# A first product from the bank behind the head norm's sums, first queries turned in their banks, another order of the low parts and of both layers: a two-layer decoder trunk on one core

## The chip, the core and the metric

One core of a Trainium2 chip. The metric is the device time of one execution in microseconds; before the change the median of three runs is 367.07 us (366.95 to 367.86). Engines are named as in the profile: PE (TensorE, its weight loads PEld), DVE (VectorE), ACT (ScalarE), POOL (GpSimd), SP (the queue that issues the weights' DMAs).

## The reference, cut to what matters

256 tokens of 1024 features go through two layers; each adds a mixer's output, then a gated per-layer embedding.

```python
def rms_norm(x, gain):
    y = xf * lax.rsqrt(jnp.mean(xf * xf, axis=-1, keepdims=True) + NORM_EPS)
def rope(x, pos):
    x1, x2 = xf[..., :half], xf[..., half:]
    return concatenate([x1 * cos - x2 * sin, x2 * cos + x1 * sin])
def moba_layer(h, w_in, q_gain, k_gain, w_out, pos):          # layer 0
    q, k, v, z = split(h @ w_in, 4)
    q = rope(rms_norm(split_heads(q, 16), q_gain), pos)       # a norm per head of 64
    k = rope(rms_norm(split_heads(k, 16), k_gain), pos)
    o = merge_heads(moba_attention(q, k, v)) * silu(z)
    return o @ w_out
def nsa_layer(...):                                           # layer 1
    q, kc, vc, ks, vs, kw, vw, gl, z = split(h @ w_in, offs)
    # q, ks, kw: head norm and rope as above; kc, vc compressed by an MLP;
    # three attention branches (compressed, selected, window), mixed by sigmoid(gl)
for i in range(2):
    x = x + mixer_i(rms_norm(x, norm_gain[i]))
    gate = sigmoid(rms_norm(x, ple_gate_gain[i]) @ ple_w_gate[i])
    x = x + gate * (p[i] @ ple_w_proj[i])
```

## The kernel before, in words

**Products in three parts.** Every float32 matrix is split into a high part rounded to TensorE's fast float32 format (ACT, `hi`; for activations `ah`) and the rest (DVE, `lo` and `al`: raw minus high), and a product is three matmuls: high by high, high by low, low by high (`split` L465, `split_act` L477, `Unit.mul` L506). So each weight tile that SP fetches into one of five `raw` buffers costs one ACT and one DVE instruction before PE can finish its share; the `raw` buffer is free for the next DMA when DVE has made `lo`.

**Layer 0.** The first queries (`uq0`, L750) are computed while x and the first weights arrive: the loop at L765 takes the eight k-tiles x0 to x7. Then `moba_half` (L792) makes keys (`uk`) and values (`uv`) for the first eight heads, and once more queries, keys and values for the other eight; the string HALVES sets in which order these steps are recorded. `qe` and `ke` copy a product out of its PSUM banks by ACT (`rope_evac`), so that the banks come free; `q` and `k` call `rope`. The attention of the first eight heads runs between the second half's products.

**The head norm and rope** (`rope`, L605). ACT squares, DVE sums (`ssq`), DVE adds epsilon (`r0`, shown as r), POOL raises the 128x16 numbers to the power -1/2 (`r_q`, `r_k`), and DVE multiplies by sine and cosine tables: two half products with the halves exchanged into a buffer `qs` (shown as tmp), one full product, one sum per token half t. For queries DVE negates the result (`nr_q`); for keys it multiplies by it. What feeds the products is the PSUM bank (`mm`), or, if an evacuation was recorded, the copy in SBUF (`q`, `k`).

**What sets the order.** Nothing runs in the order of the text: a planner (`Plan`, L85) records all operations with their dependencies, gives each a cost, and lays them out on the engines in list-scheduling order; the program then holds five fixed queues. Earlier recorded operations win among ready ones. HALVES and ORDER (for layer 1: KE and QE0/QE1 are the ropes, KT the transposes and low parts of the keys, vs/vw/kc/q1 projections, S, T, V, A, b, c pieces of the attention of group 0 to 3) set the order of recording; BEHIND tells behind which weight loads the constants' DMAs stand; `hold` keeps an operation behind another's start, and `together` (L219) makes a run of operations stand next to each other.

Of the kernel before, what the change touches and what calls it, by code (L numbers as in the profile page):

```python
# [7 lines left out]
F32 = mybir.dt.float32  # L8
# [5 lines left out]
P = 128  # L14
# [6 lines left out]
NRAW, NHI, NLO, NPT, NA = 5, 5, 5, 9, 9  # L21
WARM = 16
MARGIN = 100.0
ORDER = ("vw vs VS KE KT QE0 0A 0S1 0S0 0T0 0S3 kc 0T1 0S2 0T2 1A 0T3 q1.0 1S0 VW 1T0 1S2 q1.1 KC W0 0V q1.2 W1 "
         "1S3 q1.3 1T3 QE1 2A W2 1T2 W3 1S1 WE 2S2 2S0 0c 1T1 1V 2T2 0b 1c 2T0 3A 2S1 2c 2T1 2S3 3S1 3c 1b 2T3 3S0 "
         "2V 2b 3T0 3T1 3S2 3T2 3S3 3T3 3V 3b")

HALVES = ("k0 consts k1 norm qe k2 k3 v0 tabs masks v1 v2 q v3 k v", "k0 k1 k2 k3 q v0 k v1 v2 v3 v")

BEHIND = "0 3"  # L30
CST, CST_N = {}, 0
for _k, _n in (("ident", 128), ("cos", 128), ("sin", 128), ("mask", 384), ("cmask", 32), ("valid", 2), ("rmask", 4),
               ("cosc", 64), ("sinc", 64), ("repl", 256)):
# [51 lines left out]
class Plan:  # L85
# [77 lines left out]
    def cost(self, op, views, first):  # L163
        n = first.elems() if isinstance(first, View) else 0
        e, m = op.engine, op.method
        if m == "dma_start":
            v = first if isinstance(first, View) else op.args[1]
            return v.elems() * 4 * v.ap.ap[0][1]
        if e == "tensor":
            k, c = op.args[1].ap.ap[0][1], op.args[1].ap.ap[1][1]  # L170
            op.mode = tuple(128 if x > 64 else 64 if x > 32 else 32 for x in (k, c))
            if m == "transpose":
                return 109.2
            if op.args[1].ap.dtype == mybir.dt.bfloat16:
                return n / 2.4
            if op.args[1].ap.dtype == F32R:
                return (n + 32) / 2.4 if n > 128 else 110

            return 2 * max(54.6 if op.mode == (128, 64) else 109.2, 2 * n / 2.4 / (2 if op.mode == (128, 64) else 1))
        if e == "gpsimd":  # L180
            if op.kwargs.get("op") == OP.pow:
                return POW + 130.0 * n
            return 100 + 2.3 * n
        psum = any(self.tags[v.tile.tag]["psum"] for v in views)
        rows = first.ap.ap[0][1]
        half = 110 if rows in (60, 64) and (any(v.box()[0] != first.box()[0] for v in views)
                                            or psum and first.ap.dtype == F32R and m == "activation") else 0
        if e == "scalar":
            if first.tile.tag == "early":
                return 1500.0  # L190
            c = (60 if psum else 110) + 0.833 * max(n, op.args[1].elems())
            return half + c + 93 * sum(isinstance(op.kwargs.get(k), View) for k in ("scale", "bias", "accum_out"))
        if m == "tensor_tensor_reduce":
            return 130 + 1.04 * n
        if m == "reciprocal":
            return 65 + 6.9 * n
        if m == "tensor_reduce":
            return 65 + 1.04 * op.args[1].elems()
        two = len([v for v in views if v.elems() > 2 and v is not first]) > 1
# [197 lines left out]
def trunk(ctx: ExitStack, tc: tile.TileContext, a, out):  # L397
# [14 lines left out]
    def tmp(name):  # L412
        return work.tile([P, 512], F32, tag="tmp", name=name, bufs=5)
# [63 lines left out]
    def split_act(src, gain=None, either=False):  # L477
        hi = apool.tile([P, T], F32R, tag="ah", name="ah")
        lo = apool.tile([P, T], F32R, tag="al", name="al")
        if gain is None:  # L480
            nc.scalar.activation(hi, src, AF.Copy)
            nc.vector.tensor_tensor(lo, src, hi.bitcast(F32), op=OP.subtract)
        else:
            if either:
                nc.copy(hi, src, gain)
            else:
                nc.scalar.activation(hi, src, AF.Copy, scale=gain)
            nc.vector.scalar_tensor_tensor(lo, src, gain, hi.bitcast(F32), op0=OP.mult, op1=OP.subtract)
        return hi, lo
# [115 lines left out]
    def rope(ps, tab, nb, norm, is_q, tag, bufs, o=None):  # L605
        if o is None:
            o = work.tile([P, 2, 512], F32, tag=tag, name=tag, bufs=bufs)
        else:
            ps = [o[:, t] for t in range(2)]
        o = o.rearrange("p t (h d) -> p t h d", d=HD)  # L610
        ssq = work.tile([P, 2, 8], F32, tag="ssq", name="ssq")
        for t in range(2):
            sq = tmp("hsq").rearrange("p (h d) -> p h d", d=HD)
            nc.scalar.activation(sq.rearrange("p h d -> p (h d)"), ps[t], AF.Square)
            nc.vector.tensor_reduce(ssq[:, t], sq, axis=AX.X, op=OP.add)
        r0 = work.tile([P, 2, 8], F32, tag="r0", name="r0")
        for t in range(2):
            nc.vector.tensor_scalar(r0[:, t], ssq[:, t], 1.0 if is_q else 1.0 / HD,
                                    norm.e2[:, 0 if is_q else 1, t:t + 1], op0=OP.mult, op1=OP.add)
        r = work.tile([P, 2, 8], F32, tag="r_" + tag, name="r_" + tag, bufs=bufs)  # L620
        nc.gpsimd.tensor_tensor(r.rearrange("p t h -> p (t h)"), r0.rearrange("p t h -> p (t h)"), neg_half, op=OP.pow)
        if is_q:
            nr = work.tile([P, 2, 8], F32, tag="nr_" + tag, name="nr_" + tag, bufs=bufs)
            nc.vector.tensor_scalar(nr, r, -1.0, None, op0=OP.mult)
        for t in range(2):
            v = ps[t].rearrange("p (b g d) -> p b g d", b=nb, d=HD)
            g = 8 // nb

            def tb(i, lo, hi):
                return tab[:, i, t, :, None, lo:hi].to_broadcast([P, nb, g, hi - lo])  # L630

            qs = tmp("qs").rearrange("p (b g d) -> p b g d", b=nb, d=HD)
            ot = o[:, t].rearrange("p (b g) d -> p b g d", b=nb)
            nc.vector.tensor_tensor(qs[:, :, :, 0:32], v[:, :, :, 32:64], tb(1, 0, 32), op=OP.mult)
            nc.vector.tensor_tensor(qs[:, :, :, 32:64], v[:, :, :, 0:32], tb(1, 32, 64), op=OP.mult)
            nc.vector.tensor_tensor(ot, v, tb(0, 0, HD), op=OP.mult)
            nc.vector.tensor_tensor(ot, ot, qs, op=OP.add)
            if not is_q:
                nc.vector.tensor_tensor(o[:, t], o[:, t], r[:, t, :, None].to_broadcast([P, 8, HD]), op=OP.mult)
        return o, (nr if is_q else None)  # L640
# [121 lines left out]
    nc.scalar.activation(consts.tile([P, 16], F32, name="early"), neg_half, AF.Exp)  # L762
    for o, i in zip(nc.ops[since + 1:], range(since, len(nc.ops))):
        o.after.append(i)
    for k in range(KT):  # L765
        if k:
            nc.sync.dma_start(xT[:, k], a["x"][:, k])
        x0.append(split_act(xT[:, k], ng[:, 0, k:k + 1], k == 0))
        if k == 0:
            ws = [split(None, (1, 256), True, raw) for raw in halves]  # L770
            for part in ((0, 1), (2,)):
                for c, w in enumerate(ws):
                    for b in range(2):
                        uq0.mul(w, 0, 0, b, cols=(256 * c, 256 * c + 256), parts=part)
            continue
        c0, raw = 512 * (k % 2), second if k == 1 else None
        if k >= 4:

            if not c0:
                pair = wpool.tile([P, 1024], F32, tag="raw", name="raw", bufs=NRAW)  # L780
            raw = pair[:, c0:c0 + 512]
            nc.sync.dma_start(raw, a["moba_in"][0, k // 2, :, c0:c0 + 512])
        since = len(nc.ops)
        w = split(a["moba_in"][0, k // 2, :, c0:c0 + 512], (1, 512), small=k < 4, raw=raw)
        if k == 1:

            nc.hold(since, since - 2)
        for b in range(2):
            uq0.mul(w, 0, k, b)
    tab, held_at = [], []  # L790

    def moba_half(h):  # L792
# [11 lines left out]
        def norm():  # L804

            def adds():
                for k in range(KT):
                    n0.add(k)

            nc.hold_on(adds, loads[-1] - 1)  # L810
            n0.finish()

        def tabs():
# [21 lines left out]
        for step in HALVES[h].split():  # L835
            if step in parts:
                parts[step]()
            else:
                loads.append(len(nc.ops))
                {"k": uk, "v": uv}[step[0]].step(int(step[1]))  # L840
# [537 lines left out]
```

## Time and profile before

| | us |
|---|---|
| median of three runs | 367.07 |
| the profiled execution, whole | 367.55 |
| its span, first to last instruction | 365.8 |
| PE busy | 356.0 |
| DVE busy | 324.3 |
| ACT busy | 268.8 |
| POOL busy | 33.7 |

[...] All but a few operations pass through one helper and so carry one line, L375; they are told apart by tile names. Busy time is the union of an engine's instructions, and a matmul's shown duration overlaps the next one's, so for PE the distance from start to start is the price of one.

### The profile page before, as it was taken

How to read it: one execution, taken by the hardware profiler on the slowest of the kernel's cores; microseconds unless marked ns; L12 is line 12 of the kernel's file. 1: busy time of each engine (PE TensorE's matmuls, PEld its weight loads, DVE VectorE, ACT ScalarE, POOL GpSimd, SP SyncE). 2: the span in 40 equal slices, each digit the busy share in tenths (PEclk: the TensorE clock that was granted, in tenths of full speed). 3: DMA queues.
4: the chain of work that ended last, by engine and by line, in shares of the span. 5: the costliest groups of instructions: out<-in, count | busy, mean ns of one | idle time of the engine just before them, and what ended most of it. 6: DMA issues, size and time to landing. Idle time of an engine off the chain costs nothing.

```text
span 365.8 us, 7124 instructions
## 1 busy us (share of the span) xinstructions
PE 356.0 (97%) x2569; PEld 322.0 (88%) x2569; DVE 324.3 (89%) x799; ACT 268.8 (73%) x591; POOL 33.7 (9%) x26
## 2 busy tenths in 40 slices
PE   7998999999999999999999999999999999999994
PEld 5776788789999999999888998877998998999994
DVE  4896999999799987789979999989999999687964
ACT  4874677778688886745944887979976999966711
POOL 1054300330000000010013300003000000000010
PEclk9999999999999999999999999999999999999998
DMA  7985574334732644065364854065775100273102
GB/s 241 341 300 184 212 247 156 107 125 139 265 119 103 211 175 148 28 213 190 96 205 125 282 178 159 18 224 191 276 226 202 64 2 8 109 279 126 58 30 86
DMA packets 20051, 58.97 MB, mean 161 GB/s; under 512 B 2480, under 2 KB 5296, under 8 KB 20016
## 3 DMA queue, kind: packets, MB, share of 16 engines
q1 hardware_dynamic: 19440, 58.04, 46.3%
q10 hardware_dynamic: 576, 0.48, 0.4%
q8 instruction: 20, 0.33, 0.4%
q14 instruction: 15, 0.12, 0.1%
HBM read 57.46 MB, written 1.05 MB: 160 GB/s over the span
## 4 chain that ended last, share of the span: by engine, by line
PE 82%; DVE 8%; DMA 3%; POOL 2%; issue 2%; ACT 1%; SPq 0%; ACTq 0%; DVEq 0%
PE mm L375 61%; PE tr L375 12%; PE s L375 9%; DVE lo L375 2%; POOL r_q L375 2%; DMA xT<-in_x 2%; DMA tmp<-in_moba_in 1%; DVE q L375 1%; ACT hi L375 1%; DVE tmp L375 1%; DVE vcB L375 1%; SPq L375 0%; DVE k_1r L375 0%; DVE kd_0r L375 0%; DVE hl L375 0%
## 5 line engine op out<-in xcount | busy, mean ns | idle before, releaser
L375 DVE TENSOR_TENSOR lo<-raw,hi 128x1024 fp32r<-128x1024 f32 (+2 forms) x100 | 114.4, 1159 | 5.2 <-ACT hi L375 4.8
L375 PE MATMUL mm<-al,hi 128*128 128x256 f32 x416 | 118.2, 286 | 0.0
L375 PE MATMUL mm<-ah,lo 128*128 128x256 f32 x416 | 118.1, 286 | 0.0
L375 PE MATMUL mm<-ah,hi 128*128 128x256 f32 x416 | 117.5, 287 | 0.0
L375 ACT ACTIVATE hi<-raw 128x1024 fp32r<-128x1024 f32 (+2 forms) x100 | 98.2, 1005 | 24.9 <-PE mm L375 15.2
L375 PEld LDWEIGHTS mm<-al,hi 128*128 128x128 f32 x416 | 79.6, 191 | 0.4
L375 PEld LDWEIGHTS mm<-ah,lo 128*128 128x128 f32 x416 | 79.4, 191 | 0.2
L375 PEld LDWEIGHTS mm<-ah,hi 128*128 128x128 f32 x416 | 78.8, 191 | 0.5 <-issue 0.2
L375 PE MATMUL mm<-lo,ah 128*128 128x512 f32 (+2 forms) x178 | 65.3, 376 | 2.3 <-DVE lo L375 2.3
L375 PE MATMUL mm<-hi,ah 128*128 128x512 f32 (+2 forms) x178 | 66.5, 377 | 0.8 <-DVE hi L375 0.6
L375 PE MATMUL mm<-hi,al 128*128 128x512 f32 (+2 forms) x178 | 66.3, 374 | 0.3 <-DVE al L375 0.3
L375 ACT ACTIVATE sm<-sm,nb 128x128 f32<-128x128 f32 (+1 forms) x96 | 42.7, 448 | 7.6 <-DVE nb L375 7.3
L375 PEld LDWEIGHTS mm<-lo,ah 128*128 128x128 f32 x178 | 33.2, 188 | 8.1 <-DVE lo L375 3.3
L375 PEld LDWEIGHTS mm<-hi,ah 128*128 128x128 f32 x178 | 33.6, 190 | 7.0 <-ACT hi L375 0.9
L375 PEld LDWEIGHTS mm<-hi,al 128*128 128x128 f32 x178 | 33.7, 190 | 5.9 <-DVE al L375 0.8
L375 DVE CUSTOM_DVE_ANT_0 sm<-s,cst,nr_q 128x128 f32<-128x128 f32 (+1 forms) x96 | 35.4, 411 | 2.2 <-PE s L375 1.9
L375 POOL TENSOR_TENSOR r_q<-r,neg_half 128x16 f32<-128x16 f32 x5 | 19.8, 3961 | 82.1 <-DVE r L375 82.1
L375 ACT ACTIVATE pt<-tr 128x384 f32<-128x384 f32 x48 | 22.0, 483 | 4.9 <-PE tr L375 4.6
L375 PE MATMUL tr<-cst,sm 128*128 128x128 f32 x144 | 24.4, 277 | 0.0
L375 ACT ACTIVATE ah<-xT,gain_in 128x256 fp32r<-128x256 f32 x31 | 14.4, 498 | 12.5 <-DVE xT L375 9.3
L375 ACT ACTIVATE tmp<-tmp 128x512 f32<-128x512 f32 (+3 forms) x22 | 11.2, 516 | 13.8 <-DVE tmp L375 13.8
L375 POOL TENSOR_TENSOR rstd<-ms,neg_half 128x2 f32<-128x2 f32 x4 | 4.9, 1236 | 176.1 <-DVE ms L375 176.1
(172 smaller groups left out, 545.3 us busy)
## 6 DMA issues: line engine op xcount, KB each, us to landing
raw<-in_moba_in SPq DMA_DIRECT2D x28, 512.0 KB, 4.6
raw<-in_nsa_in SPq DMA_DIRECT2D x24, 512.0 KB, 4.3
raw<-in_w_out SPq DMA_DIRECT2D x16, 512.0 KB, 3.9
raw<-in_ple_gate SPq DMA_DIRECT2D x16, 512.0 KB, 3.6
raw<-in_w SPq DMA_DIRECT2D x8, 512.0 KB, 4.4
raw<-in_ple_proj SPq DMA_DIRECT2D x4, 512.0 KB, 4.5
raw<-in_nsa_vs SPq DMA_DIRECT2D x4, 304.0 KB, 3.1
xT<-in_x SPq DMA_DIRECT2D x8, 128.0 KB, 4.3
```

The source lines that it names most:

```text
L375: getattr(getattr(self.nc, o.engine), o.method)(*[real(x) for x in o.args], **{k: real(x) for k, x in o.kwargs.items()})
```

## The change

1. `rope` records the first exchanged half product of token half 0 (`turn(0, 0)`) together with the two `r0` operations, ahead of POOL's power.
2. HALVES has no `qe` in the first half any more: the first queries are turned from their banks (mm); the second half has `qe` and `ke` (evacuated queries and keys). The eight x steps are now steps of HALVES.
3. In the first eight steps each weight's `lo` is held behind the start of the same step's `al`.
4. The strings HALVES, BEHIND and ORDER are others; the planner's cost of the 128x16 power falls by 1000 ns, which also moves operations. Group 3 adds its compressed branch inside its last products (B instead of b).

```diff
-ORDER = ("vw vs VS KE KT QE0 0A 0S1 0S0 0T0 0S3 kc 0T1 ...
-HALVES = ("k0 consts k1 norm qe k2 k3 v0 tabs masks v1 v2 q v3 k v", "k0 k1 k2 k3 q v0 k v1 v2 v3 v")
-BEHIND = "0 3"
+ORDER = ("KE vs vw KT VS QE0 0A VW 0S1 0S0 0S3 0T1 0T0 0S2 kc 0T2 ...
+HALVES = ("x0 x1 x2 x3 x4 x5 x6 x7 k0 consts norm k1 k2 tabs k3 masks v0 v1 v2 v3 v q k",
+          "k0 k1 qe q k2 k3 v0 ke k v1 v2 v3 v")
+BEHIND = "0 2"
...
             if op.kwargs.get("op") == OP.pow:
-                return POW + 130.0 * n
+                return (POW if n < 16 else 1300.0) + 130.0 * n
...
+        def turn(t, c):
+            lo, hi = 32 * c, 32 * c + 32
+            nc.vector.tensor_tensor(qss[t][:, :, :, lo:hi], vs[t][:, :, :, 32 - lo:64 - lo], tb(1, t, lo, hi), op=OP.mult)
+
+        since = len(nc.ops)
         for t in range(2):
             nc.vector.tensor_scalar(r0[:, t], ssq[:, t], 1.0 if is_q else 1.0 / HD,
                                     norm.e2[:, 0 if is_q else 1, t:t + 1], op0=OP.mult, op1=OP.add)
+
+        turn(0, 0)
+        nc.together(since)
         r = work.tile([P, 2, 8], F32, tag="r_" + tag, name="r_" + tag, bufs=bufs)
         nc.gpsimd.tensor_tensor(r..., r0..., neg_half, op=OP.pow)
...
         for t in range(2):
-            nc.vector.tensor_tensor(qs[:, :, :, 0:32], v[:, :, :, 32:64], tb(1, 0, 32), op=OP.mult)
-            nc.vector.tensor_tensor(qs[:, :, :, 32:64], v[:, :, :, 0:32], tb(1, 32, 64), op=OP.mult)
-            nc.vector.tensor_tensor(ot, v, tb(0, 0, HD), op=OP.mult)
-            nc.vector.tensor_tensor(ot, ot, qs, op=OP.add)
+            if t:
+                turn(t, 0)
+            turn(t, 1)
+            nc.vector.tensor_tensor(ot, vs[t], tb(0, t, 0, HD), op=OP.mult)
+            nc.vector.tensor_tensor(ot, ot, qss[t], op=OP.add)
...
-    for k in range(KT):
+    def first(k):
...
         x0.append(split_act(xT[:, k], ng[:, 0, k:k + 1], k == 0))
+        low = len(nc.ops) - 1
...
+        nc.hold(len(nc.ops) - 1, low)
...
-            nc.hold_on(adds, loads[-1] - 1)
+            nc.hold_on(adds, len(nc.ops) - 1)
```

The amount of work is the same: the program has as many matmuls of every shape as before, and DVE and ACT exchange a few copies (the planner picks the engine for some).

**First place: DVE at the first queries' rope** (layer 0, while PE works on the first keys). lo is the low part of a weight; raw_119, raw_120, raw_116 and raw_117 hold, in this order, the second, third and fourth weight of the first keys and the first weight of the values; mm_78 and mm_79 are the queries' two banks. Before:

```order
L375 TENSOR_SCALAR r_0_137<-ssq_135,e_0_128 128x8 x2
L375 TENSOR_TENSOR tmp_83<-q_131,tq_0_133 128x8x32
L375 TENSOR_TENSOR lo_112<-raw_120,hi_107 128x1024
L375 TENSOR_TENSOR tmp_83<-q_131,tq_0_133 128x8x32
L375 TENSOR_TENSOR tmp_84<-q_131,tq_0_133 128x8x32
L375 TENSOR_TENSOR lo_113<-raw_116,hi_108 128x1024
L375 TENSOR_TENSOR q_131<-q_131,tq_0_133 128x512
L375 TENSOR_TENSOR tmp_84<-q_131,tq_0_133 128x8x32
L375 TENSOR_TENSOR q_131<-q_131,tmp_83 128x512
L375 TENSOR_SCALAR nr_q_141<-r_q_139 128x16
L375 TENSOR_TENSOR q_131<-q_131,tq_0_133 128x512
L375 TENSOR_TENSOR lo_114<-raw_117,hi_109 128x1024
```

With the change (numbers of buffers are shifted by three; raw_123, raw_119 and raw_120 are the keys' third and fourth and the values' first weight):

```order
L376 TENSOR_SCALAR r_0_139<-ssq_137,e_0_128 128x8 x2
L376 TENSOR_TENSOR tmp_83<-mm_78,tq_0_131 128x8x32
L376 TENSOR_TENSOR lo_115<-raw_123,hi_110 128x1024
L376 TENSOR_TENSOR tmp_83<-mm_78,tq_0_131 128x8x32
L376 TENSOR_TENSOR q_135<-mm_78,tq_0_131 128x512
L376 TENSOR_TENSOR tmp_84<-mm_79,tq_0_131 128x8x32
L376 TENSOR_TENSOR q_135<-q_135,tmp_83 128x512
L376 TENSOR_TENSOR lo_116<-raw_119,hi_111 128x1024
L376 TENSOR_SCALAR nr_q_143<-r_q_141 128x16
L376 TENSOR_TENSOR tmp_84<-mm_79,tq_0_131 128x8x32
L376 TENSOR_TENSOR q_135<-mm_79,tq_0_131 128x512
L376 TENSOR_TENSOR lo_117<-raw_120,hi_112 128x1024
```

The products now read the banks instead of the SBUF copy. Between the negation nr_q and the values' first low part stood one full product; now a half product and a full one.

**Second place: DVE in the first steps.** hi_108 is the second weight's high part, lo_113 its low part, al_98 the low part of x1. Before:

```order
L375 CAST hi_108<-tmp_84 128x512
L375 TENSOR_TENSOR lo_113<-tmp_84,hi_108 128x512
L375 SCALAR_TENSOR_TENSOR al_98<-xT_63,gain_in_64,ah_89 128x256
```

With the change:

```order
L376 CAST hi_111<-tmp_84 128x512
L376 SCALAR_TENSOR_TENSOR al_101<-xT_63,gain_in_64,ah_92 128x256
L376 TENSOR_TENSOR lo_116<-tmp_84,hi_111 128x512
```

The low part of x1 goes ahead of the weight's; the steps behind already had this order.

**Third place: DVE at the start of layer 1's attention.** k_0r, k_1r, v_0r (before v_1r) and kd_0r are the keys' low parts of the four groups (each x2), hl the low part of the first group's queries, lo_113 to lo_115 (before) and lo_116 to lo_118 (now) the second to fourth weight of kc. Before:

```order
L375 TENSOR_TENSOR k_0r<-tr_76,k_0r 64x512 x2
L375 TENSOR_TENSOR k_1r<-tr_76,k_1r 64x512 x2
L375 TENSOR_SCALAR nr_q_141<-r_q_140 128x16
L375 TENSOR_TENSOR q_132<-q_132,tmp_83 128x512
L375 TENSOR_TENSOR lo_113<-raw_116,hi_108 128x1024
...
L375 TENSOR_TENSOR lo_115<-raw_118,hi_110 128x1024
L375 TENSOR_TENSOR v_1r<-tr_75,v_1r 64x512 x2
L375 TENSOR_TENSOR kd_0r<-tr_75,kd_0r 64x512 x2
L375 TENSOR_TENSOR hl_149<-tr_76,hl_149 64x512 x2
```

With the change:

```order
L376 TENSOR_TENSOR k_0r<-tr_76,k_0r 64x512 x2
L376 TENSOR_TENSOR k_1r<-tr_76,k_1r 64x512 x2
L376 TENSOR_TENSOR v_0r<-tr_75,v_0r 64x512 x2
L376 TENSOR_TENSOR kd_0r<-tr_75,kd_0r 64x512 x2
L376 TENSOR_SCALAR gt_178<-gt_178 128x48
L376 TENSOR_TENSOR q_136<-q_136,tmp_83 128x512
L376 TENSOR_SCALAR gt_178<-gt_178,cst_65 128x16
L376 TENSOR_TENSOR lo_116<-raw_119,hi_111 128x1024
L376 TENSOR_TENSOR lo_117<-raw_120,hi_112 128x1024
L376 TENSOR_TENSOR lo_118<-raw_121,hi_113 128x1024
L376 TENSOR_TENSOR hl_149<-tr_76,hl_149 64x512 x2
```

All eight low parts of the keys now stand ahead of kc's second low part; the whole keys' part also begins earlier in the layer (KE is recorded first, and the projections vs and vw have changed places).

## Rows read from the trace of the kernel before

**Rows 1.** The page's head: the span, and per engine the busy time, its share and the instructions.

```profile
span 365.8 us, 7124 instructions
PE 356.0 (97%) x2569; PEld 322.0 (88%) x2569; DVE 324.3 (89%) x799; ACT 268.8 (73%) x591; POOL 33.7 (9%) x26
```

**Rows 2.** The view of waits, for PE and for DVE: engine and tile that waited, what it waited for; us in total, times, longest.

```profile
PE mm L375 <- DVE lo L375: 2.3, 3, 1.7
...
DVE nr_q L375 <- POOL r_q L375: 2.8, 1, 2.8
```

**Rows 3.** Busy time by stretch: the stretch and its length, then PE, PEld, DVE, ACT, POOL busy (and instructions), granted clock, DMA share, GB/s.

```profile
45.00:200.00 155.00, 155.00 (x1095) 141.85 (x1094) 141.03 (x310) 113.92 (x231) 11.62 (x5) 1.00 0.46 154
```

**Rows 4.** The chain of waits that ended last, in order of time, at the first queries' rope and at a run of transposes: start, us, what.

```profile
23.28 7.50 POOL r_q L375
...
68.04 2.04 PE tr L375 x20
```

**Rows 5.** POOL in order of time: start, us, line, operation, tiles; in brackets idle time and what ended it.

```profile
20.32 0.71 POOL L375 TENSOR_TENSOR rstd<-ms,neg_half 128x2 f32<-128x2 f32 x1 [18.81 <-DVE ms L375]
23.28 7.49 POOL L375 TENSOR_TENSOR r_q<-r,neg_half 128x16 f32<-128x16 f32 x1 [2.25 <-DVE r L375]
...
38.45 2.90 POOL L375 TENSOR_TENSOR r_k<-r,neg_half 128x16 f32<-128x16 f32 x1 [6.64 <-DVE r L375]
...
159.71 1.62 POOL L375 TENSOR_TENSOR rstd<-ms,neg_half 128x2 f32<-128x2 f32 x1 [79.26 <-DVE ms L375]
...
252.46 2.90 POOL L375 TENSOR_TENSOR r_q<-r,neg_half 128x16 f32<-128x16 f32 x1 [45.43 <-DVE r L375]
```

**Rows 6.** DVE in order of time from the first queries' sums on.

```profile
22.85 0.36 DVE L375 TENSOR_SCALAR r<-ssq,e 128x8 f32<-128x8 f32 x2
23.11 0.42 DVE L375 TENSOR_TENSOR tmp<-q,tq 128x256 f32<-128x256 f32 x1
23.45 1.22 DVE L375 TENSOR_TENSOR lo<-raw,hi 128x1024 fp32r<-128x1024 f32 x1
24.58 0.75 DVE L375 TENSOR_TENSOR tmp<-q,tq 128x256 f32<-128x256 f32 x2
...
26.39 0.68 DVE L375 TENSOR_TENSOR q<-q,tq 128x512 f32<-128x512 f32 x1
26.99 0.42 DVE L375 TENSOR_TENSOR tmp<-q,tq 128x256 f32<-128x256 f32 x1
27.33 0.68 DVE L375 TENSOR_TENSOR q<-q,tmp 128x512 f32<-128x512 f32 x1
30.81 0.26 DVE L375 TENSOR_SCALAR nr_q<-r_q 128x16 f32<-128x16 f32 x1 [2.80 <-POOL r_q L375]
```

**Rows 7.** DVE beside other powers of POOL (compare the times with rows 5).

```profile
38.28 0.42 DVE L375 TENSOR_TENSOR tmp<-mm,tk 128x256 f32<-128x256 f32 x1
...
159.55 1.21 DVE L375 TENSOR_TENSOR lo<-raw,hi 128x1024 fp32r<-128x1024 f32 x1
160.68 0.24 DVE L375 TENSOR_SCALAR e<-ms 128x2 f32<-128x2 f32 x2
160.83 1.21 DVE L375 TENSOR_TENSOR lo<-raw,hi 128x1024 fp32r<-128x1024 f32 x1
...
252.22 1.41 DVE L375 TENSOR_TENSOR tmp<-mm,tq 128x256 f32<-128x256 f32 x4
253.55 1.29 DVE L375 TENSOR_TENSOR q<-q,tmp 128x512 f32<-128x512 f32 x2
```

**Rows 8.** PE in order of time at its stops in layer 0.

```profile
8.11 0.50 PE L375 MATMUL mm<-hi,al 128*128 128x512 f32 x1 [0.33 <-DVE al L375]
...
16.28 0.50 PE L375 MATMUL mm<-hi,ah 128*128 128x512 f32 x1
...
30.60 0.39 PE L375 MATMUL mm<-hi,ah 128*128 128x512 f32 x1
30.83 0.39 PE L375 MATMUL mm<-hi,al 128*128 128x512 f32 x1
32.95 0.50 PE L375 MATMUL mm<-lo,ah 128*128 128x512 f32 x1 [1.74 <-DVE lo L375]
...
43.88 0.33 PE L375 MATMUL tr<-cst,k 128*128 128x128 f32 x1
44.48 0.33 PE L375 MATMUL tr<-cst,k 128*128 128x128 f32 x1 [0.28 <-DVE k L375]
```

**Rows 9.** ACT, then DVE, at the last of the eight x steps.

```profile
14.67 0.51 ACT L375 ACTIVATE ah<-xT,gain_in 128x256 fp32r<-128x256 f32 x1 [1.45 <-DMA xT<-in_x]
...
15.61 0.61 ACT L375 ACTIVATE hi<-raw 128x512 fp32r<-128x512 f32 x1
...
15.22 0.48 DVE L375 SCALAR_TENSOR_TENSOR al<-xT,gain_in,ah 128x256 fp32r<-128x256 f32 x1 [1.13 <-ACT ah L375]
```

**Rows 10.** Layer 1: DVE at the start of its attention, and PE where it stopped there and before the first compressed scores (kcB).

```profile
207.96 1.38 DVE L375 TENSOR_TENSOR k_0r<-tr,k_0r 64x512 fp32r<-64x512 f32 x2
...
219.47 0.28 PE L375 MATMUL mm<-ah,lo 128*128 128x256 f32 x1
219.80 0.94 PE L375 MATMUL s<-k_0r,hl 128*128 128x256 f32 x4
...
279.45 0.41 PE L375 MATMUL s<-kcB,qk_0r 128*128 128x32 f32 x2 [0.33 <-DVE nb L375]
```

More of the change, by code (lines that the diff above doesn't have):

```diff
@@ L23 @@
 MARGIN = 100.0
-ORDER = ("vw vs VS KE KT QE0 0A 0S1 0S0 0T0 0S3 kc 0T1 0S2 0T2 1A 0T3 q1.0 1S0 VW 1T0 1S2 q1.1 KC W0 0V q1.2 W1 "
-         "1S3 q1.3 1T3 QE1 2A W2 1T2 W3 1S1 WE 2S2 2S0 0c 1T1 1V 2T2 0b 1c 2T0 3A 2S1 2c 2T1 2S3 3S1 3c 1b 2T3 3S0 "
-         "2V 2b 3T0 3T1 3S2 3T2 3S3 3T3 3V 3b")
-HALVES = ("k0 consts k1 norm qe k2 k3 v0 tabs masks v1 v2 q v3 k v", "k0 k1 k2 k3 q v0 k v1 v2 v3 v")
-BEHIND = "0 3"
+ORDER = ("KE vs vw KT VS QE0 0A VW 0S1 0S0 0S3 0T1 0T0 0S2 kc 0T2 1A 0T3 q1.0 1S0 q1.1 KC 1T0 q1.2 W0 1S2 W1 0V "
+         "1S3 q1.3 W2 1S1 W3 QE1 1T2 2A 1T3 WE 1T1 2S2 0c 2S0 2S3 1c 1V 2T0 2T2 0b 2T3 2S1 2T1 2c 3A 3S0 1b 3S1 2V "
+         "3S3 2b 3c 3T0 3S2 3T3 3B 3T1 3T2 3V")
+HALVES = ("x0 x1 x2 x3 x4 x5 x6 x7 k0 consts norm k1 k2 tabs k3 masks v0 v1 v2 v3 v q k",
+          "k0 k1 qe q k2 k3 v0 ke k v1 v2 v3 v")
+BEHIND = "0 2"
 CST, CST_N = {}, 0
@@ L616, in rope, with tb @@
         r0 = work.tile([P, 2, 8], F32, tag="r0", name="r0")
+        g = 8 // nb
+        qss = [tmp("qs").rearrange("p (b g d) -> p b g d", b=nb, d=HD) for _ in range(2)]
+        vs = [ps[t].rearrange("p (b g d) -> p b g d", b=nb, d=HD) for t in range(2)]
+        def tb(i, t, lo, hi):
+            return tab[:, i, t, :, None, lo:hi].to_broadcast([P, nb, g, hi - lo])
+        def turn(t, c):
+            lo, hi = 32 * c, 32 * c + 32
+            nc.vector.tensor_tensor(qss[t][:, :, :, lo:hi], vs[t][:, :, :, 32 - lo:64 - lo], tb(1, t, lo, hi), op=OP.mult)
+        since = len(nc.ops)
         for t in range(2):
@@ L625, in rope @@
         for t in range(2):
[L626 to L632, printed above, removed]
-            ot = o[:, t].rearrange("p (b g) d -> p b g d", b=nb)
-            nc.vector.tensor_tensor(qs[:, :, :, 0:32], v[:, :, :, 32:64], tb(1, 0, 32), op=OP.mult)
-            nc.vector.tensor_tensor(qs[:, :, :, 32:64], v[:, :, :, 0:32], tb(1, 32, 64), op=OP.mult)
-            nc.vector.tensor_tensor(ot, v, tb(0, 0, HD), op=OP.mult)
-            nc.vector.tensor_tensor(ot, ot, qs, op=OP.add)
+            ot = o[:, t].rearrange("p (b g) d -> p b g d", b=nb)
+            if t:
[3 more added lines that the diff above has]
+            nc.vector.tensor_tensor(ot, ot, qss[t], op=OP.add)
             if not is_q:
@@ L764, in trunk @@
         o.after.append(i)
-    for k in range(KT):
+    pair = [None]
+    def first(k):
         if k:
@@ L774, in trunk @@
                         uq0.mul(w, 0, 0, b, cols=(256 * c, 256 * c + 256), parts=part)
-            continue
+            return
         c0, raw = 512 * (k % 2), second if k == 1 else None
@@ L779, in trunk @@
             if not c0:
-                pair = wpool.tile([P, 1024], F32, tag="raw", name="raw", bufs=NRAW)
-            raw = pair[:, c0:c0 + 512]
+                pair[0] = wpool.tile([P, 1024], F32, tag="raw", name="raw", bufs=NRAW)
+            raw = pair[0][:, c0:c0 + 512]
             nc.sync.dma_start(raw, a["moba_in"][0, k // 2, :, c0:c0 + 512])
@@ L785, in trunk @@
         if k == 1:
-            nc.hold(since, since - 2)
+            nc.hold(since, low - 1)
+        nc.hold(len(nc.ops) - 1, low)
         for b in range(2):
@@ L837, in moba_half @@
                 parts[step]()
+            elif step[0] == "x":
+                first(int(step[1]))
             else:
```

## The prediction, on record before the changed kernel ran

> **What bounds the kernel now.** I read the page's head first: PE is busy for 356.0 of 365.8 us, DVE for 324.3, ACT for 268.8, POOL for 33.7 [rows 1]. The work of PE is the same after the change, so only PE's stops can be won; the rest is a floor. The table of busy time by stretch says where there are none: from 45 to 200 us PE is busy for all of the 155 us [rows 3]. The view of waits names the largest that is left: products that wait for DVE's lo, 2.3 us in three waits, the longest 1.7, while DVE itself waits 2.8 us for POOL's r_q in one piece [rows 2]. The chain of waits has POOL's part of it on the path, at the first queries' rope: from 23.28 for 7.50 us [rows 4]. PE's rows there: the values' first products start at 30.60 and 30.83, one every 0.23 us, so the next was due at 31.06; it starts at 32.95 and takes 0.50 us instead of 0.39 [rows 8]. That stop costs 1.89 + 0.11 = 2.0 us.
>
> **Why the power took 7.5 us.** The same operation, 128x16, takes 2.90 us at 38.45 and at 252.46; only at 23.28 it takes 7.49 [rows 5]. What differs is DVE beside it. From 23.11 to 28.0 DVE runs without a gap through products and low parts whose two inputs both lie in SBUF (tmp<-q,tq; lo<-raw,hi; q<-q,tmp) [rows 6], and 28.0 + 2.9 is 30.9, just about the end of the power at 30.77. At 38.45 and 252.46 DVE read a PSUM bank instead (tmp<-mm) [rows 5, 7]. The small power tells the same: 0.71 us at 20.32; 1.62 us at 159.71, where a low part ran until 160.68 and then two scalar operations for 0.15 us: 160.68 + 0.71 = 161.39, it ended at 161.33 [rows 5, 7]. So a power waits as long as DVE runs two-input operations from SBUF, and 0.15 us of anything else lets it in.
>
> **The change, part by part.**
>
> *Bank product behind the sums, first queries from the banks.* With the change the half product right behind the r pair reads the bank, as at 38.28. The power that was asked for at 23.28 should start there and end at 26.18. If it misses that gap of 0.34 us it finds the next two bank products from 24.58 on, and ends at 27.48. DVE's queue behind the r pair, with the prices of rows 6 by starts (half product 0.34, full product or sum 0.60, low part 1.13): half 23.45, low part 24.58, half 24.92, full 25.52, half 25.86, sum 26.46, low part 27.59. There stands nr_q, and the power is done in either case: the wait of 2.80 us goes. Behind nr_q come 0.17 for itself, a half product, a full one and the values' first low part: 27.76, 28.10, 28.70, 29.83. PE wants it at 31.06, so 1.2 us are to spare: the stop of 2.0 us goes. The banks are held longer, until 28.70; the values' first product into the second bank is due three products behind 30.60, at 31.3: free. The two copies of the queries that ACT no longer makes are worth nothing: DVE's queue, not ACT, set the time of the sums, as 22.85 follows without a gap on the low part before it.
>
> *The keys behind them.* DVE stays ahead by the 2.8 us that it no longer waits, PE by 2.0. At 43.88 to 44.48 PE stops between two transposes of the keys, 0.60 us from start to start [rows 8], where a transpose takes 0.10 (2.04 us for 20) [rows 4]: 0.5 us. In the new order eight products of 0.23 us stand between these two, while DVE reaches the keys' last product 0.8 us earlier against PE than before: the stop goes. Gain 0.5 us. Late next would be the queries' and keys' parts for the first scores, with 17 products ahead of them instead of 23; by DVE's queue they are ready about 0.3 us before PE wants them.
>
> *Order of the first low parts.* PE's first product with al waits 0.33 us at 8.11 [rows 8]. Earlier al saves about 0.45 us there, up to x6. But x7 lands so late that its ah starts at 14.67, the last hi at 15.61, and PE goes on at 16.28 [rows 8, 9]; behind it DVE runs the same operations in the same order from 15.22 [rows 9]. So this is costed at nothing: x7's DMA covers it. Were x7 earlier, it would be worth 0.45 us, which is the upper end.
>
> *SP, constants.* The second load of constants goes ahead of the keys' fourth weight and puts it back by about one load; DVE's low part of it now stands 1.1 us later in its queue. Nothing.
>
> *Second half of layer 0.* Four more copies by ACT, about 0.55 us each, minus nothing: ACT is busy for 113.9 of the 155 us there [rows 3]. The first half product now reads SBUF, but attention's bank readers stand right behind it, so the power gets in 0.3 us later; nobody waits for it at once. Nothing.
>
> *Layer 1.* PE's stops there are small: 0.33 us from 219.47 to 219.80 where 0.12 is the pace, and 0.33 idle before 279.45 [rows 10]: at most 0.5 us to win. Against it: ahead of kc's second low part DVE has all eight low parts of the keys, 0.70 us each [rows 10], 5.6 us in one piece, where four stood before. Adding up DVE's queue from the second norm on by these prices, that low part comes about 0.4 us after PE wants it. No row shows this order. It is bounded by half a microsecond won, from these stops, and by 1.9 us lost, the largest stop for a low part in this trace [rows 8]. I take 0, nearer to the small stops, since a low part was late by more than half a microsecond only once in this trace [rows 2, 8].
>
> **Sum.** 2.0 + 0.5 + 0 = 2.5 us. The profiled execution took 367.55 us (span 365.8), which would become 365.05; it lies 0.48 above the median of the runs, 367.07, which would become 364.6. What a measurement can tell from no change is about 0.3%, 1.1 us.
>
> **Rivals.**
>
> *POOL holds what DVE needs.* The power gets in at 23.28, and now DVE is shut out: the low part at 23.45 starts at 26.18, all behind it 2.73 us later. The keys' third weight then has its low part at 27.4, where PE wants it at about 25.6 (24 products of 0.23 before 30.60, third product): a stop of 1.8 us in place of the 2.0. With the keys' 0.5 won, 0.7 us: 366.4. Against it: at 253.55 two sums with both inputs in SBUF take 1.29 us together in the midst of the power of 252.46 to 255.36, and a low part beside the small power takes 1.21 at 160.83, not slower than 1.22 at 23.45 [rows 5, 6, 7]. Chance 0.05. [...]
>
> *The first long power is slow whatever DVE does.* It ends at 30.77 again; behind nr_q stand 0.34 us more than before, so PE goes on 0.3 us later than 32.95. With the keys' 0.5 us: 366.9, no change. Against it: the first small power of all, at 20.32, is the fastest of its kind [rows 5]. Chance 0.07.
>
> *Layer 1 gives a part back.* A stop of 0.4 to 1.9 us at kc's second low part: 365.0 to 366.5. For it, my own sum; against it, that all its terms are uncertain by as much. Chance 0.12.
>
> *Slower.* One mechanism: the sigmoid's gt on DVE waits for ACT's tanh of the vs products; behind it stand the queries' half product, whose bank PE needs for vw, and all of the keys' low parts. If the tanh comes late on ACT, behind a high part whose weight has not landed, PE, DVE and ACT wait for each other in a ring. The sum has the ring closing with about 0.1 us to spare; it turns the sign from 2.5 us on and is measurable from 3.6 us. At 4 us: 368.6. Chance 0.06.
>
> **Numbers.** Forecast 0.70 (363.5 to 365.7: from 0.45 at the x steps and 0.5 in layer 1 won, to 1.1 lost in layer 1), all of it faster by over 0.3%; of the partial giving back two thirds are faster, the rest no change. Faster 0.70 + 0.08 = 0.78, same 0.04 + 0.05 + 0.07 = 0.16, slower 0.06. The range reaches from the lower end of the forecast to the rival with POOL, 363.5 to 366.4.
>
> **What would show it.** Right: the first r_q takes 2.9 to 4.3 us, DVE has no wait for r_q, PE's products follow each other from 30.6 to the first scores without a stop over 0.3 us; PE waits as before up to 23 us. Wrong: r_q at 7 us again; or DVE's low part at 23.45 is stretched or late by more than 2 us; or PE stops for lo at kc, near 214 us of the new time, for more than 1 us. The prediction fails if stops of layer 1 add up to more than 1.4 us above those shown.

## The result and the profile after

| | before | with the change |
|---|---|---|
| median of four runs each, us | 367.17 | 364.62 |
| their range, us | 366.95 to 367.86 | 364.08 to 365.40 |
| span of the profiled execution, us | 365.8 | 362.8 |

The ratio is 0.9929, 95% interval 0.9906 to 0.9952: faster by 0.7%, 364.62 us where 364.6 was forecast. The sum came out; its parts did so less well, as the ledger below shows.

The page's head after. As in [rows 1], PE's busy time stands still and its stops shrink; POOL is busy for 27.9 us instead of 33.7.

```profile
span 362.8 us, 7126 instructions
PE 355.8 (98%) x2569; PEld 322.5 (89%) x2569; DVE 325.6 (90%) x807; ACT 268.9 (74%) x584; POOL 27.9 (8%) x26
```

The view of waits, all that PE still waits for (us in total, times, longest). In [rows 2] lo stood at 2.3 us with a longest of 1.7; and DVE's wait for r_q is gone from the view.

```profile
PE tr L376 <- DVE ones L376: 1.1, 1, 1.1
PE mm L376 <- DVE lo L376: 0.9, 3, 0.4
PE mm L376 <- DVE hi L376: 0.2, 1, 0.2
PE mm L376 <- ACT hi L376: 0.2, 1, 0.2
```

POOL in order of time: the first queries' power takes 2.91 us where [rows 5] has 7.49; the small one at 155.86, behind a low part as before, still takes 1.62.

```profile
22.58 2.91 POOL L376 TENSOR_TENSOR r_q<-r,neg_half 128x16 f32<-128x16 f32 x1 [2.25 <-DVE r L376]
...
155.86 1.62 POOL L376 TENSOR_TENSOR rstd<-ms,neg_half 128x2 f32<-128x2 f32 x1 [79.48 <-DVE ms L376]
```

DVE beside it, to be read against [rows 6]: a bank product starts at 22.42 and the power at 22.58; the low part at 22.75 runs inside the power and is as long as ever, 1.21. The negation at 26.88 has no wait, and the values' first low part starts at 27.89.

```profile
22.15 0.35 DVE L376 TENSOR_SCALAR r<-ssq,e 128x8 f32<-128x8 f32 x2
22.42 0.41 DVE L376 TENSOR_TENSOR tmp<-mm,tq 128x256 f32<-128x256 f32 x1
22.75 1.21 DVE L376 TENSOR_TENSOR lo<-raw,hi 128x1024 fp32r<-128x1024 f32 x1
23.89 0.41 DVE L376 TENSOR_TENSOR tmp<-mm,tq 128x256 f32<-128x256 f32 x1
...
26.88 0.16 DVE L376 TENSOR_SCALAR nr_q<-r_q 128x16 f32<-128x16 f32 x1
...
27.89 1.21 DVE L376 TENSOR_TENSOR lo<-raw,hi 128x1024 fp32r<-128x1024 f32 x1
```

PE in order of time: the product that stopped from 30.83 to 32.95 [rows 8] is the 127th of PE's matmuls in both kernels; it now stands at 30.34, 0.23 behind the one before it. Between the two transposes of the keys, at 40.98 and 42.95, there are eight products and no stop. At 212.75 is a new stop, for kc's second low part. The transposes of the sums of squares (sqacc) open the norms, and serve as marks of the stages below.

```profile
18.24 0.50 PE L376 MATMUL tr<-ones,sqacc 128*128 128x2 f32 x4
...
30.11 0.39 PE L376 MATMUL mm<-hi,al 128*128 128x512 f32 x1
30.34 0.39 PE L376 MATMUL mm<-lo,ah 128*128 128x512 f32 x1
...
40.98 0.27 PE L376 MATMUL tr<-cst,k 128*128 128x128 f32 x1
...
42.95 0.27 PE L376 MATMUL tr<-cst,k 128*128 128x128 f32 x1
...
155.00 0.39 PE L376 MATMUL tr<-ones,sqacc 128*128 128x2 f32 x3
...
182.88 0.39 PE L376 MATMUL tr<-ones,sqacc 128*128 128x2 f32 x3
...
212.11 0.28 PE L376 MATMUL mm<-al,hi 128*128 128x256 f32 x1
212.75 0.74 PE L376 MATMUL mm<-ah,lo 128*128 128x256 f32 x4 [0.36 <-DVE lo L376]
...
343.27 0.39 PE L376 MATMUL tr<-ones,sqacc 128*128 128x2 f32 x3
```

DVE ahead of that stop: eight low parts of the keys, 5.6 us in one piece, and only then kc's second to fourth.

```profile
204.99 1.38 DVE L376 TENSOR_TENSOR k_0r<-tr,k_0r 64x512 fp32r<-64x512 f32 x2
206.38 1.40 DVE L376 TENSOR_TENSOR k_1r<-tr,k_1r 64x512 fp32r<-64x512 f32 x2
207.81 1.38 DVE L376 TENSOR_TENSOR v_0r<-tr,v_0r 64x512 fp32r<-64x512 f32 x2
209.21 1.40 DVE L376 TENSOR_TENSOR kd_0r<-tr,kd_0r 64x512 fp32r<-64x512 f32 x2
...
211.48 3.48 DVE L376 TENSOR_TENSOR lo<-raw,hi 128x1024 fp32r<-128x1024 f32 x3
```

**The ledger.** This table splits the gain by stage. The four marks of PE (sqacc, in the trace of before at 18.87, 158.84, 186.73 and 345.96) give the length of each stage in us, by differences. The columns on the right are experiments of the next section.

| stage | before | change | change again | e8 | e8 again | e9 |
|---|---|---|---|---|---|---|
| to the first sums of squares | 18.87 | 18.24 | 18.80 | 18.31 | 18.00 | 17.49 |
| layer 0 | 139.98 | 136.76 | 136.74 | 136.90 | 136.61 | 136.64 |
| its gate | 27.88 | 27.88 | 27.88 | 27.89 | 27.89 | 27.88 |
| layer 1 | 159.23 | 160.39 | 160.23 | 158.93 | 158.92 | 158.94 |
| the rest | 19.80 | 19.56 | 19.55 | 19.80 | 19.80 | 19.81 |

So the change won 0.63 us at the start and 3.22 in layer 0, lost 1.16 in layer 1 and won 0.24 at the end: 2.93. The trace of before has a stop of 0.33 us in layer 1, at 279.45 [rows 10], that e8 does not have; against e8's 158.93 and 158.92 layer 1 lost 1.3 to 1.5 us.

### The profile page after: what moved, and what is told of

The parts are those of the page before. It is cut to its first block, busy times and chain, and to the rows that moved or that the text cites. A ratio compares the mean times of both kernels' runs of the same rounds, so it can differ in the third digit from the quotient of the medians.

```text
span 362.8 us, 7126 instructions
## 1 busy us (share of the span) xinstructions
PE 355.8 (98%) x2569; PEld 322.5 (89%) x2569; DVE 325.6 (90%) x807; ACT 268.9 (74%) x584; POOL 27.9 (8%) x26
## 3 DMA queue, kind: packets, MB, share of 16 engines
HBM read 57.46 MB, written 1.05 MB: 161 GB/s over the span
## 4 chain that ended last, share of the span: by engine, by line
PE 89%; ACT 3%; DMA 3%; DVE 2%; issue 1%; SPq 0%; ACTq 0%; DVEq 0%
PE mm L376 67%; PE tr L376 12%; PE s L376 10%; DMA xT<-in_x 2%; DMA tmp<-in_moba_in 1%; ACT hi L376 1%; DVE lo L376 1%; ACT tmp L376 0%; SPq L376 0%; ACT k_1r L376 0%; ACT v_0r L376 0%; DVE ssq L376 0%; ACT k_0r L376 0%; ACTq L376 0%; DVE tmp L376 0%
## 5 line engine op out<-in xcount | busy, mean ns | idle before, releaser
L376 PE MATMUL mm<-ah,hi 128*128 128x256 f32 x416 | 114.8, 286 | 0.0
L376 PEld LDWEIGHTS mm<-ah,hi 128*128 128x128 f32 x416 | 77.8, 191 | 0.3 <-issue 0.2
L376 POOL TENSOR_TENSOR r_q<-r,neg_half 128x16 f32<-128x16 f32 x5 | 14.6, 2924 | 80.5 <-DVE r L376 80.5
L376 PEld LDWEIGHTS tr<-cst,sm 128*128 128x128 f32 x144 | 17.2, 141 | 2.4 <-ACT sm L376 0.4
```

Source lines behind the costliest of these rows:

```text
L376: getattr(getattr(self.nc, o.engine), o.method)(*[real(x) for x in o.args], **{k: real(x) for k, x in o.kwargs.items()})
```

## The experiments

**What lets the power in.** Each kernel here puts another operation behind the first queries' sums. For e2, e3, e7, e8 and e10 it is one more DVE operation in the kernel before, into scratch (e8 is shown; `banks` is `ps` ahead of its replacement by the SBUF copy). The planner lays the queues out anew for each of them. In e3, e7 and e8 every engine has the same operations in the same order, apart from this one; e10 shares DVE's order with them up to 45 us. All four differ from the kernel before by more than the one operation: two low parts, for example, stand earlier in DVE's queue. e2 has yet another order.

```diff
+        since = len(nc.ops)
         for t in range(2):
             nc.vector.tensor_scalar(r0[:, t], ...)
+        if not hasattr(nc, "gap"):
+            nc.gap = True
+            nc.vector.tensor_scalar(sq[..., :256], banks[0][:, :256], 1.0, None, op0=OP.mult)
+            nc.together(since)
```

e2 reads `ps[0][:, :256]` (the copy) instead, e7 all 512 columns of it; e3 multiplies its two halves, `tensor_tensor(..., ps[0][:, :256], ps[0][:, 256:], op=OP.mult)`; e10 sums it, `tensor_reduce(sq[:, 0, 0:4], ps[0][:, :256]..., op=OP.add)`. e1 and e4 are edits of the changed kernel:

```diff
-HALVES = ("x0 ... k0 consts norm k1 k2 tabs ...
+HALVES = ("x0 ... k0 consts norm qe k1 k2 tabs ...
```

```diff
-        turn(0, 0)
         nc.together(since)
...
-            if t:
-                turn(t, 0)
+            turn(t, 0)
```

What was expected, in the order e1, e2, e3, e4:

> The changed kernel, but the first queries are copied out of their banks by ACT again, so the half product right behind the sums reads SBUF on both inputs. Theory (a power waits as long as DVE runs operations with two inputs from SBUF): the first queries' power takes about 7.2 us, from 22.6 until nr_q at about 30, and PE stops for the low part behind nr_q for 1.5 to 2.2 us; 366.3 to 367.1 us. Rival (the place right behind the sums is what helps): the power takes 2.9 us, no stop, 364.6 us.

> The kernel before with one more DVE operation right behind the first queries' sums: a 128x256 multiplication by 1.0 of the SBUF copy into scratch, one input, about 0.2 us. Theory (two inputs from SBUF keep the power out, one does not): the power takes 2.9 to 3.0 us, DVE does not wait for it, PE's stop of 2.0 us goes: 364.7 to 365.5 us. Rival (only a read of a PSUM bank lets it in): 7.5 us or more, the stop stays, 367.1 to 367.5 us.

> The same place in the kernel before, but the extra operation has two inputs from SBUF (128x256, product of the two halves of the copy, about 0.42 us). Theory: the power is still kept out, 7.5 to 8.0 us, and PE's stop is 2.0 to 2.5 us; 367.1 to 367.8 us. Rival (any pause between the sums and the low part is enough): 2.9 us, 365.0 us.

> The changed kernel, but the first half product is recorded behind the power, as before, so that a low part (two inputs from SBUF, 1.2 us) stands between the sums and the first bank product. Theory: the power gets in with the first bank product, 1.2 us later, and shows 4.0 to 4.2 us, ending near 26.7; nr_q stands at about 26.9, so nobody waits: 364.6 us, as the changed kernel within 0.4 us. Rival (the power has to find the gap right behind the sums): 7 us and the stop of 2 us again, 366.6 us.

And of the second and third set, e7, e8, e10:

> The kernel before with one longer DVE operation behind the first queries' sums: a 128x512 multiplication by 1.0 of the SBUF copy, one input, about 0.45 us, so that about 0.25 us of it lie behind the moment at which the power is asked for (in the earlier variant with 128x256 that was about 0.1 us, and the power still took 7.69 us). Theory A (one input leaves the power in, 0.1 us was too short): the power takes 2.9 us, and PE's stop behind it goes. Theory B (a one-input operation from SBUF keeps it out too, only a bank read lets it in): 7.9 us and a stop of 1.3 to 2.2 us.

> The same place in the kernel before, but the extra operation, 128x256, one input, reads the queries' PSUM bank. Theory B (a bank read lets the power in): the power takes 2.9 us, DVE does not wait for it, PE's stop for the values' low part goes, so that the rest of layer 0 ends about 2 us earlier against the end of the x steps. Theory C (less than 0.2 us of any operation is too short): about 7.7 us, and the stop stays.

> The kernel before with a sum over 128x256 of the queries' SBUF copy behind their sums: one input from SBUF, as in the two variants that kept the power out, but an operation that takes 0.68 us for 512 columns where the multiplication by 1.0 took 0.41. [...] Theory B (only a bank read lets it in): 8.9 us and the stop.

| kernel | what stands behind the sums, its us | power, us | nr_q waits | PE idle for the values' low part |
|---|---|---|---|---|
| before | product, two inputs SBUF, 0.42 | 7.49 | 2.80 | 1.74 |
| e1 | product, two inputs SBUF, 0.41 | 7.50 | 2.80 | 1.77 |
| e3 | product 128x256, two inputs SBUF, 0.41 | 8.97 | 2.80 | 0.50 |
| e2 | times 1.0, 128x256, one input SBUF, 0.28 | 7.69 | 2.80 | 1.25 |
| e7 | times 1.0, 128x512, one input SBUF, 0.41 | 8.97 | 2.80 | 0.49 |
| e10 | sum, 128x256, one input SBUF, 0.41 | 2.90 | none | none |
| e8 | times 1.0, 128x256, one input a bank, 0.41 | 2.91 | none | none |
| change | product, bank and SBUF, 0.41 | 2.91 | none | none |
| e4 | low part 1.21, then product from the bank | 3.81 | none | none |

The cleanest price comes from e3, e7 and e8, whose queues are the same and whose extra operation takes 0.41 us in each. From the moment at which the power is asked for to the sums of squares behind layer 0 there are 135.17, 135.15 and 132.51 us: the blocked power costs 2.65 us. It shows at two stops of PE and in many small pieces behind the first scores. The two stops in e7, and the same two products in e8:

```profile
33.23 0.50 PE L375 MATMUL mm<-lo,ah 128*128 128x512 f32 x1 [0.49 <-DVE lo L375]
43.02 0.33 PE L375 MATMUL tr<-cst,k 128*128 128x128 f32 x1 [1.31 <-DVE k L375]
```

```profile
33.22 0.39 PE L375 MATMUL mm<-lo,ah 128*128 128x512 f32 x1
41.39 0.27 PE L375 MATMUL tr<-cst,k 128*128 128x128 f32 x1
```

So the last column of the table shows only a part of what e3 and e7 lose; the stop of 2.0 to 2.5 us that was expected for e3 came as 0.50 there and 1.32 at the keys' transposes.

What keeps the power out is told by e7 and e10. They have an operation of the same 0.41 us with one input, the same SBUF copy, in the same place. POOL, then DVE, of e7 in order of time:

```profile
22.08 8.97 POOL L375 TENSOR_TENSOR r_q<-r,neg_half 128x16 f32<-128x16 f32 x1 [2.25 <-DVE r L375]
```

```profile
21.91 0.41 DVE L375 TENSOR_SCALAR tmp<-q 128x512 f32<-128x512 f32 x1
22.25 1.21 DVE L375 TENSOR_TENSOR lo<-raw,hi 128x1024 fp32r<-128x1024 f32 x1
...
31.08 0.27 DVE L375 TENSOR_SCALAR nr_q<-r_q 128x16 f32<-128x16 f32 x1 [2.80 <-POOL r_q L375]
```

and of e10:

```profile
23.12 2.90 POOL L375 TENSOR_TENSOR r_q<-r,neg_half 128x16 f32<-128x16 f32 x1 [2.25 <-DVE r L375]
```

```profile
22.96 0.41 DVE L375 TENSOR_REDUCE tmp<-q 128x4 f32<-128x256 f32 x1
23.29 1.21 DVE L375 TENSOR_TENSOR lo<-raw,hi 128x1024 fp32r<-128x1024 f32 x1
...
29.23 0.16 DVE L375 TENSOR_SCALAR nr_q<-r_q 128x16 f32<-128x16 f32 x1
```

What fits all rows is the speed of reading SBUF: the multiplication goes through 512 columns in 0.41 us, the sum through 256, so the first reads at double speed; the two inputs of e3 are 512 columns together in 0.41 us as well, and e2 reads 256 in 0.28. That is my reading of the rows; no run shows the cause behind it. The multiplication and the sum differ in more than that (the sum is another kind of operation and writes 4 columns instead of 512), and no run keeps these apart. Either way my theory was too narrow: e2 missed, and e7 went against the theory that one input leaves the power in; e10, 2.90 us where I expected 2.9 to 3.1, in turn refutes that only a bank read lets it in. In the other direction nothing was shut out: low parts of 1.21 us ran inside the power in the changed kernel (at 22.75), e8 (22.87) and e10 (23.29), and were not longer than those ahead of it (1.21 at 21.02, 21.14 and 21.55).

In all five blocked cases nr_q waits 2.80 us behind the last of DVE's operations, however long the power had been asked for: the times are those of a 2.8 us operation that starts when DVE stops. e4 shows that the place right behind the sums is not needed here: with a low part ahead of the first bank product the power takes 3.81 us (4.0 to 4.2 expected) and still ends in time, and layer 0 takes 136.86 us.

Times: e1 366.83 us (ratio 0.9987, interval 0.9964 to 1.0011, no different from before), e2 365.86 (0.9959, 0.9945 to 0.9973; the plan moved the values' low part directly behind nr_q, so the blocked power costs PE 1.25 us instead of 1.74), e3 366.75 and e7 365.61 (one run each), e10 364.56 (one run), **e8 363.28 (0.9921, 0.9888 to 0.9955)**: one bank read of 0.41 us, with the order strings of before, brings the whole gain of layer 0. By e3 and e7 2.65 us of it are the power's; about 0.4 us are the other order of the queues, since from the request for the power to the end of layer 0 the kernel before takes 135.56 us and e7, blocked as well, 135.15.

**Orders.** e4's total is 373.0 us (1.0158, 1.0135 to 1.0180), 8 us over what was expected, and layer 0 has no part in that. PE's largest wait is in layer 1; PE, then ACT:

```profile
213.49 0.58 PE L376 MATMUL mm<-ah,hi 128*128 128x256 f32 x1 [5.81 <-ACT v L376]
```

```profile
208.14 1.17 ACT L376 ACTIVATE k_0r<-tr 64x512 fp32r<-64x512 f32 x2
...
211.74 1.20 ACT L376 ACTIVATE kd_0r<-tr 64x512 fp32r<-64x512 f32 x2
212.96 0.47 ACT L376 ACTIVATE v<-mm,rstd 128x256 f32<-128x256 f32 x1
```

PE needs a bank whose copy v stands on ACT behind all high parts of the keys. The first half product is recorded behind the power in layer 1's ropes too in this kernel, and under the new string the planner then lays the queues out differently. e5 tried the other combination, the old string under the new rope:

```diff
-ORDER = ("KE vs vw KT VS QE0 0A VW 0S1 ...
+ORDER = ("vw vs VS KE KT QE0 0A 0S1 0S0 ...
```

> The changed kernel with the layer 1 order string of the kernel before. Theory (the new order costs what the two traces differ by): from the second norm of layer 1 to the sums of squares behind it 154.9 us as in the kernel before, where the changed kernel took 156.1; 363.0 to 364.0 us. Rival (a string fits only the program it was searched with; put onto another it makes a long wait, as the variant with the late half product had one of 5.8 us in layer 1): over 157 us for that stretch, 365.5 us or more.

371.0 us (1.0117, 1.0057 to 1.0176). The rival held: layer 1 takes 165.84 us. From the transposes that end layer 1's norm to the next sums of squares:

| us | old rope | first product behind the sums |
|---|---|---|
| old string | 154.93 (before), 154.62 (e8) | 161.54 (e5) |
| new string | 164.12 (e4) | 156.08 (change) |

String and rope belong together. So the half that was left to try has both old in layer 1: e9 records the first product behind the sums in layer 0 alone and has the old string.

```diff
+        early = not hasattr(nc, "late")
+        if early:
+            turn(0, 0)
+            nc.together(since)
...
-            if t:
+            if t or not early:
                 turn(t, 0)
...
     n2 = Norm()
+    nc.late = True
```

It ran beside the changed kernel and e8, on one chip:

> Half of the change: layer 0 as changed (first queries from their banks, first half product behind the sums, order of the low parts), layer 1 with the rope and the order string of the kernel before. Theory: layer 0 gains the 3.1 to 3.2 us, from the second norm of layer 1 to the next sums of squares it takes 154.6 to 155.2 us: 363.0 to 363.8 us. Rival (string and program no longer fit, as with the old string under the new rope, 161.5 us): over 157 us for the stretch and 365.5 us or more.

> The kernel before with the extra bank read, once more, beside the changed kernel. Theory (the whole gain is the power's; the changed layer 1 gives 1.15 us back): 363.0 to 363.8 us, faster than the changed kernel by 0.8 to 1.6 us. Rival (the difference between the two earlier medians is that of the chips): both within 0.4 us.

> The changed kernel once more, on the same chip as the next two, for their comparison: 364.3 to 365.0 us. The sums of squares of x start 4.25 us (within 0.1) behind the landing of x7 if that lands after 13.6 us, as in the four traces with this order of the low parts.

Change 364.45 us (0.9927, 0.9908 to 0.9945), e8 363.48 (0.9907, 0.9884 to 0.9931), e9 **363.39 us (0.9896, 0.9878 to 0.9913)**; the six runs of e9 lie between 362.55 and 363.74, the six of the change between 363.79 and 365.01. Half of the change beats the whole by 1.06 us, and its stretch in layer 1 takes 154.63 us, as expected. e8 is 0.97 us faster than the change, which was expected too. PE's marks in e9:

```profile
17.49 0.50 PE L376 MATMUL tr<-ones,sqacc 128*128 128x2 f32 x4
...
154.13 0.28 PE L376 MATMUL tr<-ones,sqacc 128*128 128x2 f32 x2
...
182.01 0.28 PE L376 MATMUL tr<-ones,sqacc 128*128 128x2 f32 x2
...
340.95 0.50 PE L376 MATMUL tr<-ones,sqacc 128*128 128x2 f32 x4
```

**The first steps.** e6 is the changed kernel without the hold that puts al first:

```diff
-        nc.hold(len(nc.ops) - 1, low)
```

> The changed kernel without holding each weight's low part behind the start of the same step's al. Theory (the last x load sets the start): PE stops again for 0.33 us at the first al, but the products with the last weight start no later than 0.7 us behind the landing of x7 plus the operations of ACT, as in the other traces, and the total is within 0.5 us of the changed kernel: 364.3 to 365.1 us. Rival (the order of the low parts brought the 0.63 us by which the start was shorter): the sums of squares start 0.5 to 0.7 us later against the landing of x7 than in the changed kernel; 365.2 us.

364.79 us (0.9945, 0.9921 to 0.9969), with PE's 0.33 us at the first al back. All traces together tell more: when x7 landed, and when the first sums of squares started (us).

| al first | x7 landed, sums started | low part first | x7 landed, sums started |
|---|---|---|---|
| change | 13.95, 18.24 | before | 14.65, 18.87 |
| again | 14.49, 18.80 | e10 | 14.49, 18.71 |
| e5 | 14.28, 18.50 | e8 | 14.07, 18.31 |
| e4 | 13.66, 17.93 | e7 | 13.03, 18.23 |
| e1 | 14.72, 18.96 | e6 | 12.70, 18.12 |
| e9 | 12.88, 17.49 | e8 again | 12.60, 18.00 |
| | | e3 | 13.11, 18.51 |
| | | e2 | 12.26, 17.95 |

Where x7 lands after 13.6 the sums follow 4.2 to 4.3 us behind it in either order; where it lands by 13.1 the low part first starts them at 18.0 to 18.2 (18.5 in e3, where x0 too landed 0.8 us later than in most), al first, in one trace, at 17.49. Most of that lead is lost again behind the mark: PE's 127th product starts at 29.49 us in e9 and at 29.66 in e6, and the two kernels with the old start, e7 and e8 again, reach it at 29.86 and 29.90. So the swap is worth nothing in some executions and 0.2 to 0.4 us in others (one trace stands for al first there), by when a load that both kernels issue in the same order happens to land.

## Why the prediction was right, point by point

- **The first queries' power.** Right in place, size and rows. It took 2.91 us; nr_q was forecast at 27.59 on the clock of before and stands at 26.88 + 0.63 = 27.51; the values' first low part at 28.70, now 28.52. 1.3 us were to spare before the product at 30.34 (forecast 1.2). That the stop is the power's is shown by e8 and e10 (gone with it), e1 (back with it: layer 0 139.03 us), and e3 and e7, which differ from e8 in one operation. The reason as I put it, two inputs from SBUF, was too narrow, and so was "0.15 us of anything else lets it in": 0.24 us of e7's multiplication lie behind the request, and the power stayed out.
- **The keys' transposes.** Forecast 0.5 us; the stop is gone, and the four transposes there took 1.05 us of PE's queue before (from 43.52 to 44.57) and 0.27 now. It too is the power's: e7 stops there for 1.31 us, e8 with the same queues not at all. Layer 0 gave 3.22 where these two terms made 2.5. Some 0.4 of the rest comes behind the first scores, in many small pieces: from their first product to the end of layer 0 there are 108.94 us before, 108.88 in e7 and 108.54 in e8 (108.05 with the change, where two products of 0.23 more stand ahead of the scores). So most of that is the power's as well. I had written that stretch off because PE is busy for all of it [rows 3]; such small waits do not show in busy time, since a matmul's shown duration overlaps the next one's start (0.39 us shown at 30.11 in the changed kernel, and the next one starts 0.23 behind it).
- **The low parts of the first steps.** Costed at nothing, since x7's DMA covers it; the table of landings shows just that for landings after 13.6 us. The start was 0.63 us shorter in the first trace, as x7 landed 0.70 earlier, and 0.06 in the second: that gain was luck. As a term of the change the swap is worth between 0 and 0.4 us, not measured more finely.
- **Layer 1.** The step that failed: I took 0 between 0.5 won and 1.9 lost, and it lost 1.16, 0.9 with the 0.24 that the end gives back (1.06 by the medians of the change and e9). My own sum had said that kc's second low part comes 0.4 us late, and the stop at 212.75 cost 0.52; I set the sum aside because the trace of before had few such stops. That was no reason against a sum made for an order which that trace does not show. The rest of the loss lies in four stops of 0.18 to 0.26 us and smaller ones, against 0.9 us of old ones gone; a cause for each was not sought, so beyond the 0.52 us the cause stays open.
- **The rivals.** Layer 1 gives a part back: it happened, within its bounds. POOL holds what DVE needs: refuted by the low part of 1.21 us at 22.75. A first power that is slow whatever DVE does: refuted by e8 and e10. The ring through tanh did not close in the changed kernel; in e4 PE waited 5.8 us for another copy on ACT, so the danger was of the right kind.
- **The range.** Its lower end, 363.5, does not follow from its own terms: 364.6 - 0.45 - 0.5 = 363.65. Nothing hangs on it.

So in the profiled execution the total came out because 0.7 us in layer 0 and 0.6 at the start that I did not count stood against 0.9 lost that I counted as nothing. The mechanism of the main term was right; that the sum met the median to a tenth is luck.

## What to carry to other kernels

Where a short POOL operation takes far longer in one place than in others (here 7.49 us against 2.90), look at what DVE runs in that time: one operation on a bank (or a sum) right behind the request cost 0.41 us and freed 2.8. Price each stage of a change on its own marks: here half of the change was worth 3.2 us and the other half cost about 1, and the total showed only the difference. An order string that goes with one program cost 7 to 8 us under a slightly different one (161.54 against 154.62, 164.12 against 156.08), so an edit and its order have to be measured together.

## What the runs showed of the hardware

- DVE keeps POOL's power out with one SBUF input too, where it runs through 512 columns in 0.41 us (e7, the power takes 8.97 us), and not with one at 256 columns in 0.41 us (e10, 2.90).
- POOL's power does not slow DVE's two-input operations: low parts inside it took 1.21 us (22.75 in the changed kernel), as did the one ahead of it (21.02).
- Open: how wide an operation has to be to keep the power out. The two multiplications of 2 columns from SBUF at 160.68 [rows 7], with one input each, did let the small power in, by its end 0.65 us behind their start (it took 0.71 in all at 20.32), where 256 columns (e2) kept the long one out.
- x7, 128 KB, issued at 8.0 to 8.5 us (8.30 before, 8.15 with the change), landed between 12.26 and 14.72 us in these 14 traces; with al first the first sums started at 17.49 to 18.96 us, with the low part first at 17.95 to 18.87.
- Open: of 50 runs of the kernel before one took 1230.8 us, four took 363.2 to 364.0 and the others 366.3 to 368.4. The four are at the time of e8. A gap in DVE's queue that lets the power in by chance would fit; no trace of such a run was taken.
